# One encoder layer in float32r pieces: the up projection written in another order, and twelve additions of the third pass moved to VectorE

## The chip, the core and the metric

The kernel runs on one core of a Trainium2 chip. The metric is the time of the device in microseconds (us), the median over runs. The engines are PE (TensorE, matmuls), ACT (ScalarE), DVE (VectorE), POOL (GpSimd) and SP (SyncE, which here only issues DMAs).

## The reference

One layer: RMSNorm, one input projection, neighbourhood attention and a bidirectional gated recurrence side by side, a gated merge, then the MLP that the change touches, and a last RMSNorm:

```python
m = rms_norm(h, norm_mlp[l])                                   # h: 16 + 1024 rows of 1024, float32
h = h + jnp.square(jax.nn.relu(m @ w_up[l])) @ w_down[l]       # w_up 1024 x 4096, w_down 4096 x 1024
h = rms_norm(h, norm_final)                                    # the first 16 rows are dropped
```

## The kernel before

Every float32 matrix is split into a high part, `hi`, rounded to float32r by a cast on ACT, and a low part, `lo` = value - `hi`, made by a subtraction on DVE. A product is three matmuls: hi x hi, hi x lo and lo x hi. The low part is called the cast's remainder below. `weights` (L985 to L991) does this for a block of 128 x 512 weights: the cast at L989, the remainder at L990. It takes its tiles `wh`, `wl` in turn from one or two pools, with four buffers of each in each pool.

Both products of the MLP are done by Winograd's form of Strassen's scheme: 1024 rows and 1024 input columns are cut in two by two blocks, and seven products of half the size stand in place of eight. The up projection makes 4096 columns in 16 pairs of column blocks (`Pair`, m = 0 to 15). A pair has seven products, `product_1` to `product_7`. Each is a `chain` (L687 to L694) of 12 matmuls, four slices of the depth times three, that adds into one PSUM bank. The left sides are weights: the blocks a11, a12, a22 and the sums s1 to s4 that `pair_sums` makes on DVE (L682 to L685). The right sides are blocks of the normed rows and their sums (t1 to t4), transposed by PE.

Products 1 and 2 share a bank `pa`: p1 is copied to SBUF on ACT (L1055) between them, and their sum gives u11. Products 3 and 5 share `pc`: p3 is copied on ACT (L1065) before product 5 adds to the bank. Products 6, 7 and 4 share `pb`: after each, DVE adds p1 to the bank into a tile `uv` (L1070, L1085, L1100), and only then may the next chain add to the bank. DVE adds `pc` to u1 (L1074) and to u3 (L1091), and POOL subtracts p3 from u3 (L1086). Each result is relu'd and squared on ACT (L994, L995), and POOL makes four block sums of them for the next product (L1079); all go to DRAM tiles `usp`.

The order of all engines in this stage is as written: the code stands in a block that takes the scheduling out of the framework's hands (`manual_schedule`), so each engine does its instructions in the order in which the lines are called, and waits on semaphores for the other engines. Loads of weights and stores of blocks go through SP's queue in that order too.

The stage begins while the 20 transposes of the rows' last blocks and sums (L941, with a cast at L943 and its remainder at L944) are still to be done: each stands ahead of a slice of a chain. For this, products 1 and 2 of the first three pairs (`q.early`, EARLY = 3) are done before the loop over the pairs, with weights that are loaded apart (`first_load`, `first_weights`). So an early pair has five chains in the loop and a later one seven. In the loop product 4 of a pair is done in the next pair's turn. The last pair (`q.last`) makes its block sums on DVE and no weights for a next pair, but the first two steps of the down projection (`next_step`).

The down projection takes four passes over the pairs; eight banks are added to in a pass. Each step reads a pair's block from `usp` and a block of w_down, splits both (`split` at L95 to L97: cast L96, remainder L97) and has 24 matmuls. In the third pass a step makes one more difference of weights on DVE (L1268), and rows of results are added together beside it (`side`, L1334 to L1356).

Of the kernel before, what the change touches and what calls it, by code (L numbers as in the profile page):

```python
# [13 lines left out]
ALU = mybir.AluOpType  # L14
# [34 lines left out]
def layer(ctx: ExitStack, tc: tile.TileContext, x, meta, w_in, w_na, w_hg, w_o, w_up, w_dn,  # L49
# [478 lines left out]
    with (tc.tile_pool(name="npr", bufs=1, side="right", reuse_waits="tile") as npr,  # L528
# [18 lines left out]
        for p in range(NPAIR):  # L547
# [43 lines left out]
            for b in (0, 4, 8):  # L591
                pt = bank("t", "vpt")
                m = min(4, 9 - b)
# [102 lines left out]
    def up_bank(t):  # L696
        return bank(t, t).rearrange("p a b -> p (a b)")
# [254 lines left out]
    nB = []  # L952
# [32 lines left out]
    def weights(src):  # L985
        w_pools.append(w_pools.pop(0))
        hi, lo = (a_tile(w_pools[-1], t, F32R, 4) for t in ("wh", "wl"))
        v = (lambda t: t.rearrange("p (k c) -> p k c", c=P)) if len(src.shape) == 3 else (lambda t: t)
        act.copy(v(hi), src)  # L989
        dve.tensor_tensor(v(lo), src, v(hi).bitcast(F32), op=ALU.subtract)  # L990
        return hi, lo  # L991
# [10 lines left out]

    def first_weights(m):
        first_w[m] = [weights(first_raw[m][:, q:q + 4]) for q in (0, 4)]

# [44 lines left out]

    def product_1(q, w=None, between=lambda k: None):
        q.p1, q.u11 = a_tile(upa, "p1", bufs=EARLY), a_tile(upa, "u11", bufs=EARLY)
        q.pa = up_bank("pa")
        chain(q.pa, w or q.W["a11"], nV["b11"], True, between)
        act.copy(q.p1, q.pa)  # L1055
# [6 lines left out]
    def product_3(q):  # L1062
        q.pc, q.p3 = up_bank("pc"), a_tile(upb, "p3")
        chain(q.pc, q.W["s4"], nV["b22"], True)
        act.copy(q.p3, q.pc)  # L1065

# [4 lines left out]

    def product_5(q):
        chain(q.pc, q.W["s1"], nV["t1"], False)
        dve.tensor_tensor(q.u1, q.u1, q.pc, op=ALU.add)  # L1074
        relu2(q.u1, q.u1)

# [4 lines left out]

    def product_7(q):
        q.u3 = a_tile(upb, "uv", bufs=6)
        chain(q.pb, q.W["s3"], nV["t3"], False)
        dve.tensor_tensor(q.u3, q.pb, q.p1, op=ALU.add)  # L1085
        pool.tensor_tensor(q.u3, q.u3, q.p3, op=ALU.subtract)  # L1086

        block_out(q, 2, q.u11, q.u1, ALU.subtract, usp[2][q.m][:, 1])

    def finish_u3(q):  # L1090
        dve.tensor_tensor(q.u3, q.u3, q.pc, op=ALU.add)  # L1091
        relu2(q.u3, q.u3)
        (act if q.last else sp).dma_start(usp[2][q.m][:, 0], q.u3)
        block_out(q, 0, q.u1, q.u3, ALU.add, usp[1][q.m][:, 1])
        block_out(q, 1, q.S[0], q.u11, ALU.subtract, usp[1][q.m][:, 0])

    def product_4(q):
        u2 = a_tile(upb, "uv", bufs=6)
        chain(q.pb, q.W["a22"], nV["t4"], False)
        dve.tensor_tensor(u2, q.pb, q.p1, op=ALU.add)  # L1100
        relu2(u2, u2)
        (act if q.last else sp).dma_start(usp[0][q.m][:, 1], u2)
        block_out(q, 3, u2, q.S[1], ALU.subtract, usp[3][q.m // 2][:, q.m % 2])

    first_load(0)
    first_load(1)
    first_weights(0)
    first_weights(1)
    first_load(2)
    with tc.manual_schedule(engines={e.engine for e in (pe, act, dve, pool, sp)}):  # L1110
# [21 lines left out]
        rows_.close()  # L1132
        hress.close()
# [3 lines left out]
        load_pair(1)  # L1137
        product_1(pairs[2], first_w[2][0])
        pair_sums(pairs[0])
# [30 lines left out]
        product_4(pairs[-1])  # L1170
        next_step()

# [161 lines left out]
    def side(ps_, m):  # L1334
# [4 lines left out]
        if ps_ == 2 and 4 <= m < 12:  # L1339
            j = m // 2 - 2  # L1340
            if m % 2 == 0:
                pool.tensor_tensor(acc[j, 1], acc[j, 1], c5[j], op=ALU.add)
                pool.tensor_tensor(acc[j + 4, 1], acc[j + 4, 1], c5[j], op=ALU.add)
            else:
                pool.tensor_tensor(acc[j, 1], acc[j, 1], q1[j], op=ALU.add)
                square(j, 0)
# [106 lines left out]
```

## Time and profile before

| | us |
|---|---|
| median of 3 runs (1553.54 to 1555.42) | 1555.04 |
| the profiled execution's own time | 1555.45 |
| its span, first to last instruction | 1553.7 |
| busy in it: PE, DVE, ACT, POOL | 1504.5, 1040.5, 655.1, 412.4 |

The mean granted clock of PE is 0.995 of full speed. In what follows a row of the timeline reads: start and length in us, engine, line, operation, result<-operands, shapes, and in brackets how long the engine was idle before it and who released it. A matmul's length holds its way through the array, so matmuls overlap; how dense they are is seen from their starts. A row of waits reads: who waited, for whom, us in total, times, longest. Line numbers are those of the kernel before where the time is of before; in the changed kernel L1065 has become L1066, L1070 L1072, L1074 L1076, L1100 L1102, L1079 L1082, L1185 L1195, and L1268 L1278.

### The profile page before, as it was taken

To read this page: it belongs to the slowest core of one execution; us is meant where nothing else is said; L and a number is where in the kernel's file an instruction comes from. 1 tells how busy PE (TensorE), PEld (TensorE's weight loads), DVE (VectorE), ACT (ScalarE), POOL (GpSimd) and SP (SyncE) were. 2 spreads that over 40 slices of the span, in tenths; PEclk is the share of its full clock that TensorE was granted. 3 is DMA by queue.
4 is the path that set the end of the run, shared out by engine and by line. 5 is a ranking of instruction groups with operands and counts; after the bars stand their busy time and mean duration, and the time that the engine had idled before them with its cause. 6 is when DMAs were issued, how large, how long until landed. Compare 5 with 4: busy or idle time off the path is not lost. (4 is left out here: it accounts for less than half of the span.)

```text
span 1553.7 us, 23462 instructions
## 1 busy us (share of the span) xinstructions
PE 1504.5 (97%) x9188; PEld 1252.5 (81%) x9188; DVE 1040.5 (67%) x1589; ACT 655.1 (42%) x1173; POOL 412.4 (27%) x367
## 2 busy tenths in 40 slices
PE   6999999999999999999999999899999999999998
PEld 5788888877888887888888887788888888887886
DVE  6666666664876877666485367777777544879676
ACT  6231313124666666334133244444444443433444
POOL 4313131315314400011000122444444300237132
PEclk9999999999999999999999999999999999999999
DMA  5101010103123128434746123444444576562324
GB/s 180 42 28 56 28 56 29 56 28 127 50 72 119 62 68 264 136 129 161 252 163 216 55 89 109 147 153 151 150 151 154 203 270 237 195 230 98 106 82 149
DMA packets 142591, 196.13 MB, mean 126 GB/s; under 512 B 8064, under 2 KB 90112, under 8 KB 142480
## 3 DMA queue, kind: packets, MB, share of 16 engines
q1 hardware_dynamic: 133680, 173.13, 33.8%
q10 hardware_dynamic: 6624, 14.16, 2.3%
q0 software_dynamic: 2176, 7.34, 1.3%
q8 instruction: 72, 1.18, 0.3%
q14 instruction: 39, 0.32, 0.1%
HBM read 140.08 MB, written 54.53 MB: 125 GB/s over the span
## 5 line engine op out<-in xcount | busy, mean ns | idle before, releaser
L135 PE MATMUL mm<-aT,hi 128*128 128x512 f32 (+2 forms) x640 | 229.7, 359 | 2.1 <-DVE QX L563 1.5
L137 PE MATMUL mm<-aT,lo 128*128 128x512 f32 (+2 forms) x640 | 227.5, 356 | 0.0
L136 PE MATMUL mm<-aT,hi 128*128 128x512 f32 (+2 forms) x640 | 226.3, 354 | 0.0
L135 PEld LDWEIGHTS mm<-aT,hi 128*128 128x128 f32 x640 | 121.7, 190 | 16.4 <-issue 1.7
L97 DVE TENSOR_TENSOR dl<-ur,dh 128x1024 fp32r<-128x1024 f32 x54 | 75.5, 1398 | 85.5 <-ACT dh L96 85.4
L137 PEld LDWEIGHTS mm<-aT,lo 128*128 128x128 f32 x640 | 121.5, 190 | 13.3
L136 PEld LDWEIGHTS mm<-aT,hi 128*128 128x128 f32 x640 | 121.7, 190 | 12.5
L96 ACT CAST dh<-ur 128x1024 fp32r<-128x1024 f32 x54 | 56.9, 1053 | 161.0 <-issue 78.1
L990 DVE TENSOR_TENSOR wl<-raw,wh 128x512 fp32r<-128x512 f32 x50 | 55.5, 1115 | 45.2 <-ACT wh L989 45.2
L125 ACT CAST hi<-raw 128x1024 fp32r<-128x1024 f32 x36 | 37.8, 1050 | 106.1 <-PE mm L136 75.5
L994 ACT ACTIVATE uv<-uv 128x512 f32<-128x512 f32 x48 | 30.4, 632 | 118.2 <-DVE uv L1100 66.4
L990 DVE TENSOR_TENSOR wl<-sx,wh 128x512 fp32r<-128x512 f32 x70 | 48.0, 696 | 31.8 <-ACT wh L989 31.7
L1086 POOL TENSOR_TENSOR uv<-uv,p 128x512 f32<-128x512 f32 x16 | 25.9, 1619 | 141.9 <-ACT wh L989 105.5
L1265 POOL TENSOR_TENSOR w<-w,tt 128x512 f32<-128x512 f32 x16 | 23.4, 1462 | 131.1 <-DVE tt L1264 103.4
L399 POOL TENSOR_TENSOR Y<-X,TN 128x512 f32<-128x512 f32 x20 | 33.8, 1691 | 88.8 <-DVE X L396 88.8
L692 PE MATMUL pb<-nt,wh 128*128 128x512 f32 x128 | 51.4, 402 | 6.1 <-DVE uv L1085 3.8
L126 DVE TENSOR_TENSOR lo<-raw,hi 128x1024 fp32r<-128x1024 f32 x34 | 45.9, 1349 | 16.1 <-ACT hi L125 16.0
L618 DVE CUSTOM_DVE_ANT_0 pr<-nsc,NB 128x432 f32<-128x432 f32 (+1 forms) x64 | 35.2, 559 | 27.2 <-PE nsc L613 27.0
L92 POOL TENSOR_SCALAR rtm<-ssq 128x1 f32<-128x1 f32 (+1 forms) x17 | 6.6, 391 | 173.3 <-ACT junk L920 159.2
L692 PE MATMUL pa<-nT,wh 128*128 128x512 f32 x128 | 51.5, 402 | 0.7 <-ACT p L1055 0.7
L1175 PE MATMUL mm<-dl,dh 128*128 128x512 f32 x124 | 49.1, 396 | 1.9 <-DVE dl L97 1.9
L135 PE MATMUL mm<-wh,mT 128*128 128x512 f32 x128 | 50.2, 392 | 0.0
(380 smaller groups left out, 4449.8 us busy)
## 6 DMA issues: line engine op xcount, KB each, us to landing
raw<-in_w_in SPq DMA_DIRECT2D x56, 512.0 KB, 4.0
ur<-usp SPq DMA_DIRECT2D x54, 512.0 KB, 3.5
raw<-in_w_up SPq DMA_DIRECT2D x16, 1024.0 KB, 6.6
usp<-us SPq DMA_DIRECT2D x60, 256.0 KB, 4.6
sg<-gsp SPq DMA_DIRECT2D x16, 512.0 KB, 3.7
w<-in_w_dn SPq DMA_DIRECT2D x16, 512.0 KB, 4.6
usp<-uv SPq DMA_DIRECT2D x30, 256.0 KB, 5.7
gsp<-gv ACTq DMA_DIRECT2D x24, 256.0 KB, 2.6
```

What stands on the lines that cost most here:

```text
L96: act.copy(hi, src)
L97: dve.tensor_tensor(lo, src, hi.bitcast(F32), op=ALU.subtract)
L125: act.copy(hi[:, :kc], raw[:, :kc])
L126: eng.tensor_tensor(lo[:, :kc], raw[:, :kc], hi[:, :kc].bitcast(F32), op=ALU.subtract)
L135: pe.matmul(ps, lh, rh, start=first, stop=False)
L136: pe.matmul(ps, lh, rl, start=False, stop=False)
L137: pe.matmul(ps, ll, rh, start=False, stop=last)
L399: pool.tensor_tensor(fap(Y, h, mid3), fap(X, h, mid3), fap(TT, 0, [[4, g], [n + 3, 2], [0, h]]), op=ALU.mult)
L618: dve.tensor_tensor_reduce(out=pr[:, :w], in0=sc[:, :w], in1=NB[:, i, o:o + w], scale=1.0, scalar=3.0e38, op0=ALU.add, op1=ALU.min, accum_ ...
L692: pe.matmul(ps, lhs[0][:, c], rhs[0][:, k], start=first and k == 0, stop=False, skip_group_check=True)
L990: dve.tensor_tensor(v(lo), src, v(hi).bitcast(F32), op=ALU.subtract)
L1175: pe.matmul(ps, a[n == 2][:, q, j * P:(j + 1) * P], b[n == 1][:, q], start=first and n == 0, stop=last and n == 2, skip_group_check=True)
```

## The change

1. *p1 - p3 ahead, in the result's tile.* p3 is copied into the tile of u3, and POOL makes u3 = p1 - u3 there at once (L1066, L1067). After product 7 DVE adds `pb` (L1087) and `pc` (L1088). Before, DVE added p1 to `pb` (L1085), POOL subtracted p3 (L1086), and DVE added `pc` (L1091) in the next pair's turn.
2. *Casts ahead of activations.* The cast and remainder of s3 stand ahead of u1's relu and square, those of a22 ahead of u3's. In the early pairs s1 goes ahead of product 5. In a later pair s1 does as well. u2's relu and square come after the weights a11 and s4 (early) or ahead of product 3 (later).
3. *Block sums and loads.* A pair's first three block sums stand together behind product 7 (`pair_out`), so the next load of weights stands behind their stores in SP's queue. For the last pair they come behind product 4.
4. *Three p1 chains first.* Ahead of the loop the order is product 1 of pairs 0, 1, 2 and then product 2 of pairs 0, 1, 2. The third p1 has a bank of its own (`mm`). The first slice has no transposes ahead of it. Transposes stand in the first four chains, as before in the first four.
5. *Third pass.* Three additions for each of four row blocks go from POOL to DVE (L1342, L1343, L1345 before).

```diff
-    def first_weights(m):
-        first_w[m] = [weights(first_raw[m][:, q:q + 4]) for q in (0, 4)]
+    def first_weights(m, *halves):
+        first_w.setdefault(m, []).extend(weights(first_raw[m][:, 4 * q:4 * q + 4]) for q in halves)
...
     def product_3(q):
-        q.pc, q.p3 = up_bank("pc"), a_tile(upb, "p3")
+        q.pc, q.u3 = up_bank("pc"), a_tile(upb, "uv", bufs=6)
         chain(q.pc, q.W["s4"], nV["b22"], True)
-        act.copy(q.p3, q.pc)
+        act.copy(q.u3, q.pc)
+        pool.tensor_tensor(q.u3, q.p1, q.u3, op=ALU.subtract)
...
-    def product_5(q):
+    def product_5(q, then):
         chain(q.pc, q.W["s1"], nV["t1"], False)
         dve.tensor_tensor(q.u1, q.u1, q.pc, op=ALU.add)
+        then()
         relu2(q.u1, q.u1)
...
-    def product_7(q):
-        q.u3 = a_tile(upb, "uv", bufs=6)
+    def product_7(q, then):
         chain(q.pb, q.W["s3"], nV["t3"], False)
-        dve.tensor_tensor(q.u3, q.pb, q.p1, op=ALU.add)
-        pool.tensor_tensor(q.u3, q.u3, q.p3, op=ALU.subtract)
-
-        block_out(q, 2, q.u11, q.u1, ALU.subtract, usp[2][q.m][:, 1])
-
-    def finish_u3(q):
+        dve.tensor_tensor(q.u3, q.u3, q.pb, op=ALU.add)
         dve.tensor_tensor(q.u3, q.u3, q.pc, op=ALU.add)
+        then()
         relu2(q.u3, q.u3)
         (act if q.last else sp).dma_start(usp[2][q.m][:, 0], q.u3)
+
+    def pair_out(q):
+
+        block_out(q, 2, q.u11, q.u1, ALU.subtract, usp[2][q.m][:, 1])
         block_out(q, 0, q.u1, q.u3, ALU.add, usp[1][q.m][:, 1])
         block_out(q, 1, q.S[0], q.u11, ALU.subtract, usp[1][q.m][:, 0])
...
-        product_1(pairs[0], first_w[0][0], lambda k: transposes(1))
-        transposes(1)
+        product_1(pairs[0], first_w[0][0], lambda k: transposes(k > 0))
+        first_weights(2, 0)
+        transposes(2)
         scale_row(7, rs7)
-        product_2(pairs[0], first_w[0][1], lambda k: transposes(1))
-        nB.append(row_sums(3))
-        transposes(1)
         product_1(pairs[1], first_w[1][0], lambda k: transposes(1))
         transposes(1)
-        first_weights(2)
-        product_2(pairs[1], first_w[1][1], lambda k: transposes(1))
+        nB.append(row_sums(3))
+        product_1(pairs[2], first_w[2][0], lambda k: transposes(1), "mm")
         transposes(1)
+        product_2(pairs[0], first_w[0][1], lambda k: transposes(1))
+        transposes(1)
+        first_weights(2, 1)
+        product_2(pairs[1], first_w[1][1])
...
             (product_3 if q.early else product_1)(q)
-            if m:
-                finish_u3(pairs[m - 1])
             if m + 1 < NP:
                 pair_sums(pairs[m + 1])
             if m:
                 product_4(pairs[m - 1])
             if q.early:
                 product_6(q)
-                next_weights(m, "a11", "s4", "a12", "s2")
+                next_weights(m, "a11", "s4")
+                if m:
+                    finish_u2(pairs[m - 1])
+                next_weights(m, "a12", "s2", "s1")
             else:
+                finish_u2(pairs[m - 1])
                 product_3(q)
                 next_weights(m, "a11", "s4")
                 product_2(q)
                 next_weights(m, "a12", "s2")
                 product_6(q)
-            product_5(q)
-            next_weights(m, "s1")
-            product_7(q)
-            next_weights(m, "s3", "a22")
-        finish_u3(pairs[-1])
+                next_weights(m, "s1")
+            product_5(q, lambda: next_weights(m, "s3"))
+            product_7(q, lambda: next_weights(m, "a22"))
+            if not q.last:
+                pair_out(q)
         product_4(pairs[-1])
+        finish_u2(pairs[-1])
...
             if m % 2 == 0:
-                pool.tensor_tensor(acc[j, 1], acc[j, 1], c5[j], op=ALU.add)
+                dve.tensor_tensor(acc[j, 1], acc[j, 1], c5[j], op=ALU.add)
```

What this does to the order of single engines is shown at three places.

DVE in the turn of pair 0 and at the start of pair 1's, before (`uv` are u1, u3, u2, `wl` the remainders, `sx` the sums of the weights):

```order
L1070 TENSOR_TENSOR uv<-pb,p_9186 128x512
L990 TENSOR_TENSOR wl<-sx,wh 128x512 x2
L1074 TENSOR_TENSOR uv<-uv,pc 128x512
L990 TENSOR_TENSOR wl<-sx,wh 128x512
L1085 TENSOR_TENSOR uv<-pb,p_9186 128x512
L990 TENSOR_TENSOR wl<-sx,wh 128x512
L990 TENSOR_TENSOR wl<-raw,wh 128x512
L1091 TENSOR_TENSOR uv<-uv,pc 128x512
L682 TENSOR_TENSOR sx<-raw 128x512
```

And in the changed kernel, the same place:

```order
L1072 TENSOR_TENSOR uv<-pb,p_9186 128x512
L990 TENSOR_TENSOR wl<-sx,wh 128x512 x3
L1076 TENSOR_TENSOR uv<-uv,pc 128x512
L990 TENSOR_TENSOR wl<-sx,wh 128x512
L1087 TENSOR_TENSOR uv<-uv,pb 128x512
L1088 TENSOR_TENSOR uv<-uv,pc 128x512
L990 TENSOR_TENSOR wl<-raw,wh 128x512
L682 TENSOR_TENSOR sx<-raw 128x512
```

The third remainder (s1) has moved ahead of L1076 and s3's ahead of L1087, the second addition to u3 follows the first at once, and one remainder, not two, stands between it and the sums.

PE where the output projection ends (`mm`) and the stage begins (`pa` is the bank of p1, `pt` that of transposes), before:

```order
L137 MATMUL mm<-wh_8478,mT_8427 128x512
L941 MATMUL pt<-ident,hres_8493 128x128 x4
L692 MATMUL pa<-nT_8818,wh 128x512
L693 MATMUL pa<-nT_8819,wh 128x512
L694 MATMUL pa<-nT_8818,wl 128x512
```

and in the changed kernel:

```order
L137 MATMUL mm<-wh_8478,mT_8427 128x512
L692 MATMUL pa<-nT_8818,wh 128x512
L693 MATMUL pa<-nT_8819,wh 128x512
L694 MATMUL pa<-nT_8818,wl 128x512
L941 MATMUL pt<-ident,hres_8493 128x128 x4
```

Three matmuls of the first chain now stand ahead of the first four transposes.

DVE in the third pass, two steps (`hr` are rows of the result, `w` the difference of weights), in the changed kernel; before, the same place holds only the rows of L1268 (now L1278) and L97:

```order
L97 TENSOR_TENSOR dl<-w_5_12065,dh 128x1024
L1352 TENSOR_TENSOR hr<-hr,c_11988 128x512
L1353 TENSOR_TENSOR hr<-hr,c_11988 128x512
L1278 TENSOR_TENSOR w_6_12109<-w_6_12109 128x512
L97 TENSOR_TENSOR dl<-ur,dh 128x1024
L97 TENSOR_TENSOR dl<-w_6_12109,dh 128x1024
L1355 TENSOR_TENSOR hr<-hr,q_11984 128x512
L1278 TENSOR_TENSOR w_7_12149<-w_7_12149 128x512
```

Two additions have come into one step and one into the next.

More of the change, by code (lines that the diff above doesn't have):

```diff
@@ L1049, in next_weights, with product_1 @@
                 q.W[v] = weights(q.A[v])
-    def product_1(q, w=None, between=lambda k: None):
+    def product_1(q, w=None, between=lambda k: None, tag="pa"):
         q.p1, q.u11 = a_tile(upa, "p1", bufs=EARLY), a_tile(upa, "u11", bufs=EARLY)
-        q.pa = up_bank("pa")
+        q.pa = up_bank(tag)
         chain(q.pa, w or q.W["a11"], nV["b11"], True, between)
@@ L1097, in product_4, with finish_u2 @@
     def product_4(q):
-        u2 = a_tile(upb, "uv", bufs=6)
+        q.u2 = a_tile(upb, "uv", bufs=6)
         chain(q.pb, q.W["a22"], nV["t4"], False)
[L1100 to L1103, printed above, removed]
+        dve.tensor_tensor(q.u2, q.pb, q.p1, op=ALU.add)
+    def finish_u2(q):
+        relu2(q.u2, q.u2)
+        (act if q.last else sp).dma_start(usp[0][q.m][:, 1], q.u2)
+        if q.last:
+            pair_out(q)
+        block_out(q, 3, q.u2, q.S[1], ALU.subtract, usp[3][q.m // 2][:, q.m % 2])
     first_load(0)
     first_load(1)
-    first_weights(0)
-    first_weights(1)
+    first_weights(0, 0, 1)
+    first_weights(1, 0, 1)
     first_load(2)
@@ L1137, in layer @@
         load_pair(1)
-        product_1(pairs[2], first_w[2][0])
         pair_sums(pairs[0])
@@ L1341, in side @@
             if m % 2 == 0:
-                pool.tensor_tensor(acc[j, 1], acc[j, 1], c5[j], op=ALU.add)
-                pool.tensor_tensor(acc[j + 4, 1], acc[j + 4, 1], c5[j], op=ALU.add)
+                dve.tensor_tensor(acc[j, 1], acc[j, 1], c5[j], op=ALU.add)
+                dve.tensor_tensor(acc[j + 4, 1], acc[j + 4, 1], c5[j], op=ALU.add)
             else:
-                pool.tensor_tensor(acc[j, 1], acc[j, 1], q1[j], op=ALU.add)
+                dve.tensor_tensor(acc[j, 1], acc[j, 1], q1[j], op=ALU.add)
                 square(j, 0)
```

1 line of the change is left out of this document (added).

## The prediction

> **What bounds the kernel now.** I read the page first, then the waits of the matmul engine (PE), then its timeline by stage.
>
> ```profile
> span 1553.7 us, 23462 instructions
> ...
> PE 1504.5 (97%) x9188; PEld 1252.5 (81%) x9188; DVE 1040.5 (67%) x1589; ACT 655.1 (42%) x1173; POOL 412.4 (27%) x367
> ```
>
> PE is busy for 97% of the span, so an edit can save what PE loses by waiting, and only if nothing else becomes late. The waits of PE in the stages that the change touches (us in total, times, longest):
>
> ```profile
> PE pb L692 <- DVE uv L1085: 3.8, 2, 2.5
> PE pb L692 <- DVE uv L1070: 2.1, 2, 1.3
> PE mm L1175 <- DVE dl L97: 1.9, 5, 0.7
> PE pt L941 <- DVE hres L898: 0.8, 1, 0.8
> PE pa L692 <- ACT p L1055: 0.7, 1, 0.7
> PE pb L1185 <- DVE uv L1100: 0.5, 1, 0.5
> ```
>
> They hold 9.8 us, and each costs more than its row says, since PE starts slowly after one. What is really lost in the pair loop comes from PE's timeline: the first matmul of the loop, two chain starts, and the first matmul behind the last pair's product 7.
>
> ```profile
> 939.24 0.39 PE L692 MATMUL pc<-nT,wh 128*128 128x512 f32 x1
> 1226.26 0.39 PE L692 MATMUL pb<-nT,wh 128*128 128x512 f32 x1
> 1228.98 0.39 PE L692 MATMUL pc<-nt,wh 128*128 128x512 f32 x1
> 1234.42 0.39 PE L1185 MATMUL mm<-wh 128*128 128x512 f32 x1
> ```
>
> A chain of 12 matmuls takes 1228.98 - 1226.26 = 2.72 us. From 939.24 to 1234.42 PE runs 105 chains (16 pairs of seven, less products 1 and 2 of the three early pairs and less the last product 4): 105 x 2.72 = 285.6 us of work in 295.2 us. So 9.6 us are lost there, and that is the most the loop can give. Where it is lost, in the second early pair (p7, p4 and so on are the products):
>
> ```profile
> 961.31 0.50 PE L692 MATMUL pb<-nt,wh 128*128 128x512 f32 x1
> 965.21 0.63 ACT L994 ACTIVATE uv<-uv 128x512 f32<-128x512 f32 x1 [2.19 <-DVE uv L1074]
> 967.04 0.69 DVE L990 TENSOR_TENSOR wl<-sx,wh 128x512 fp32r<-128x512 f32 x1 [1.87 <-ACT wh L989]
> 967.65 0.68 DVE L1085 TENSOR_TENSOR uv<-pb,p 128x512 f32<-128x512 f32 x1
> 968.39 0.50 PE L692 MATMUL pb<-nt,wh 128*128 128x512 f32 x1 [1.31 <-DVE uv L1085]
> 970.56 0.67 DVE L1091 TENSOR_TENSOR uv<-uv,pc 128x512 f32<-128x512 f32 x1
> 971.15 1.19 DVE L682 TENSOR_TENSOR sx<-raw 128x512 f32<-128x512 f32 x1
> 974.68 1.77 DVE L685 TENSOR_TENSOR sx<-raw,sx 128x512 f32<-128x512 f32 x1
> 976.98 0.68 DVE L1070 TENSOR_TENSOR uv<-pb,p 128x512 f32<-128x512 f32 x1
> 977.71 0.50 PE L692 MATMUL pb<-nt,wh 128*128 128x512 f32 x1 [0.86 <-DVE uv L1070]
> ```
>
> Product 7 starts at 961.31 and is through by 964.0. VectorE (DVE) takes its bank over only at 967.65 (L1085), because ahead of that it waits 1.87 us for a weight cast which on ScalarE (ACT) stands behind two activations of 0.63 us each (965.21 is the first). So p4, due at 964.0 + 2.7 = 966.7, starts at 968.39. Then the four sums of the next weights take until 976.4, and L1070 at 976.98 makes p7 late (977.71). The sums are slow because of GpSimd (POOL):
>
> ```profile
> 972.65 1.57 POOL L1079 TENSOR_TENSOR us<-uv 128x512 f32<-128x512 f32 x1 [0.86 <-ACT uv L995]
> 945.50 0.69 DVE L685 TENSOR_TENSOR sx<-raw,sx 128x512 f32<-128x512 f32 x1
> 946.10 0.68 DVE L1070 TENSOR_TENSOR uv<-pb,p 128x512 f32<-128x512 f32 x1
> ```
>
> With nothing on POOL a sum takes 0.69 us (945.50). Beside POOL's work it takes 1.77 (974.68), that is 1.1 more, while L1091, which reads a PSUM bank, stays at 0.67 (970.56).
>
> **The change part by part.** I sum against the profiled execution's 1555.45 us (span 1553.7 and 1.75 around it), which lies 0.41 above the median of the three runs, 1555.04.
>
> *Pair loop.* Each pair keeps the same chains on PE, 14 DVE operations in an early pair, and five on POOL. p1 - p3 is made on POOL as soon as p3 is copied, two chains ahead of its reader or more. With time 0 at the end of p7, the early pair goes on DVE: L1087 from 0.2 (the last matmul's 0.39 less the 0.227 from one start to the next; a PSUM read, 0.67), L1088 0.67, the cast's remainder 0.69, four sums at their slow price 5.3 (971.15 to 976.4), L1102 0.68: done at 8.2. L1072 then waits for p6, which ends at 3 x 2.72 = 8.2, and is through by 9.1; p7 begins at 10.9. p4 begins at 2.72 and needs L1087, done at 0.9. Both waits that PE now has get 1.8 us of room. Three weight remainders (2.0) and L1076 follow until 11.8, s3 until 12.5, and the next L1087 is due at 13.8: DVE is in time. The casts that stand ahead of the activations cost PE nothing as long as the activations behind them, 1.3 us a time, fit into the rest of the 13.6 us (five chains): only POOL and the stores read what they make.
>
> In pairs 3 to 15 a pair has seven chains, 19.0 us, for the same sums and two more casts, so there is more room still. The copy of p1 is due at three chains, 8.2, and follows L1088 (done at 1.6), two activations (2.9) and a copy of 0.6: 3.5. If that cover went, PE would wait ahead of p2.
>
> The first pair is the exception, as no product 4 stretches it:
>
> ```profile
> 937.37 0.69 DVE L685 TENSOR_TENSOR sx<-raw,sx 128x512 f32<-128x512 f32 x1
> 938.09 1.14 ACT L989 CAST wh<-sx 128x512 fp32r<-128x512 f32 x2 [1.76 <-DVE sx L685]
> 942.67 0.58 ACT L1065 COPY p<-pc 128x512 f32<-128x512 f32 x1
> ```
>
> There POOL is free now (L1070 at 946.10 follows undisturbed sums), and p7 starts at 939.24 + 3 x 2.72 = 947.4. Afterwards POOL's p1 - p3 starts behind the copy (942.67 + 0.58) and makes one sum 1.1 longer: L1072 ends near 947.5 instead of 946.8, against a p7 that is due 0.3 earlier, at 947.1. I take 0.6 us lost there, between 0 (the operations miss each other) and 1.7 (two sums hit). Another 0.4 us I leave for slow restarts. The loop gives 9.6 - 0.6 - 0.4 = 8.6 us.
>
> *Three p1 chains first.* The first three matmuls (3 x 2.72/12 = 0.68) fill most of the 0.8 us that PE waits on L898, and the 0.7 us wait for the copy of p1 goes, since two other chains lie between. So PE could be at the loop 1.36 us earlier, at 937.9. What is late next is s4: its sum ends at 938.06 (937.37 + 0.69), its cast at 938.66. DVE starts the sums 0.7 earlier but has a weight remainder (0.6) moved ahead of them, so the sum ends near 937.95, the cast near 938.6, and with the remainder the loop starts near 938.9. Gain 0.3, from 1.3 (no wait for s4) to -0.4 (the first matmuls wait like the transposes). The extra cast in the first chain lies beside transposes.
>
> *Last pair.* L1102 and what follows it no longer stand behind three block sums, so the 0.5 us wait at L1185 goes, with its restart 0.6. Two matmuls fewer stand ahead of product 4 (4 x 0.227 = 0.9 us instead of 1.36); L1087 needs 0.9 of it. The stores of u1 and u3 wait longer, but nobody reads those blocks before later passes.
>
> *SP's queue.* The load of the next weights now stands behind two block stores, and so behind POOL.
>
> ```profile
> raw<-in_w_up SPq DMA_DIRECT2D x16, 1024.0 KB, 6.6
> ```
>
> In an early pair it goes out near 6 instead of 1 and lands 6.6 later, at 12.6 to 13; the sums that read it start at 13.6 + 2.2 = 15.8. So 2 to 3 us of cover; in the later pairs 19.0 - 13.6 = 5.4 more. I cost it at nothing.
>
> *Third pass.* POOL's twelve additions run beside DVE. First the window (length, then each engine's busy time and count, PE's first), then DVE's rows beside POOL (four) and alone (three):
>
> ```profile
> 1400.00:1450.00 50.00, 48.49 (x212) 38.98 (x211) 45.11 (x32) 21.47 (x24) 30.53 (x17) 1.00 0.30 106
> ```
>
> ```profile
> 1419.25 1.77 DVE L1268 TENSOR_TENSOR w<-w 128x512 f32<-128x512 f32 x1
> 1420.95 2.31 DVE L97 TENSOR_TENSOR dl<-ur,dh 128x1024 fp32r<-128x1024 f32 x1
> 1423.18 2.31 DVE L97 TENSOR_TENSOR dl<-w,dh 128x1024 fp32r<-128x1024 f32 x1
> 1425.41 1.77 DVE L1268 TENSOR_TENSOR w<-w 128x512 f32<-128x512 f32 x1
> 1438.16 1.22 DVE L97 TENSOR_TENSOR dl<-ur,dh 128x1024 fp32r<-128x1024 f32 x1 [0.83 <-ACT dh L96]
> 1439.30 1.22 DVE L97 TENSOR_TENSOR dl<-w,dh 128x1024 fp32r<-128x1024 f32 x1
> 1440.44 0.68 DVE L1268 TENSOR_TENSOR w<-w 128x512 f32<-128x512 f32 x1
> ```
>
> Beside POOL one step takes DVE 1425.41 - 1419.25 = 6.16 us, and PE's step of 24 matmuls is 24 x 0.227 = 5.44, so DVE sets the pace until 1436. Alone it is 1.14 + 1.14 + 0.68 = 3.0. With two additions on DVE (at most 0.7 each, as a sum) it is 4.4, with one 3.7, both under 5.44 with room even for one slowing of 1.1. In 1400 to 1450 PE made 212 matmuls where 50 / 0.227 = 220 fit: 8 x 0.227 = 1.9 us come back. POOL loses only work that nobody waits for.
>
> The page "Perfetto Trace Analysis" of the Trainium skill, section "Optimizing Scalar/DVE Operations", says of the port that the two engines share that moving operations between them "might not help". By that this term would be 0 and not 1.9; the rows of DVE alone and beside POOL speak for 1.9.
>
> Sum: 8.6 + 0.3 + 0.6 + 1.9 = 11.4. 1555.45 - 11.4 = 1544.05, and 0.41 less against the median, 1543.6; I say 1544. All waits gone and no new one would be 9.6 + 1.3 + 0.6 + 1.9 = 13.4: 1541.6. With the bad ends (1.7 in place of 0.6, -0.4 in place of 0.3) it is 9.6: 1545.4; an unseen wait of 0.1 us per pair would add 1.6: 1547.
>
> **The rivals.**
>
> 1. *The early pairs stay late* (0.12). The loads miss their 2 to 3 us of cover, or POOL hits more DVE operations than four sums. For it: an early pair moves as many bytes in 13.6 us as a later one in 19. Against: the trace's landing time above. Then the 5.9 us of the first two rows of PE's waits stay lost: 1543.6 + 5.9 = 1549.5, from 1547.5 (a third of them goes all the same) to 1550.5 (another microsecond lost elsewhere).
>
> 2. *The third pass gives nothing* (0.08), the additions being as dear on DVE as beside it: 1543.6 + 1.9 = 1545.5. The uncontended rows speak against it.
>
> 3. *Slower, by ACT's queue* (0.04). In pairs 3 to 15 eight weight tiles serve seven weights a pair, so the cast of s3 waits for p5 and that of a22 for p7, and now the activations and the copy of p1 queue behind them. The copy has 8.2 - 3.5 = 4.7 us before p2 needs it. Only from there each further microsecond costs 13 pairs one each: 13 x 1.1 = 14.3 against the 11.4 gained, 1558 (1555.04 + 2.9). It needs ACT 5.8 us behind in every pair, and nothing in the rows gives more than the 1.3 of two activations.
>
> 4. *The waits only move* (0.08): with PE closer behind, the casts are late at other chains and the loop keeps what it loses; without its 8.6 us the time is 1552.2.
>
> **How the numbers follow.** The sum has 0.68. The range takes it from 1541 (all waits gone, 1541.6, less a third of the 1.9 us between the shown runs, 1553.54 and 1555.42) up to rival 1's 1550.5. It leaves out rivals 3 and 4 and a little of the rest. About 0.2%, 3.1 us, is what a measurement of this kernel can tell from no change. Faster by more than that, under 1551.9: the sum and rivals 1 and 2, 0.88. Within it: rival 4, 0.08. Slower: rival 3, 0.04.
>
> **What would show it.** In the changed profile PE's waits on the DVE operations of p7 and p4 in pairs 1 to 3 should be gone, but for one near 0.5 us in the first pair; the loop from its first pc matmul to L1195 should last about 286.6 us; the window of the third pass should hold 219 or 220 matmuls in 50 us, with L1278 and both casts' remainders at 0.7 and 1.2. The sum is wrong if the loop still takes over 290 us, if L1072 comes later than 10.9 us behind p7's end, or if the sums wait for a load of weights.

## The result, and the profile after

The changed kernel takes 1541.29 us (median of 4 runs, 1539.05 to 1543.87) against 1555.23 before (4 runs, 1553.54 to 1555.59): a ratio of 0.9913, with a 95% interval from 0.9892 to 0.9934, so 10 to 17 us less. The profiled execution took 1543.13 us, 12.3 less than the profiled one of before; the medians differ by 13.9, and the 1.6 between them is scatter of the kind shown below. The page's first rows of the changed kernel:

```profile
span 1541.4 us, 23453 instructions
...
PE 1500.9 (97%) x9188; PEld 1253.1 (81%) x9188; DVE 1030.8 (67%) x1601; ACT 658.0 (43%) x1173; POOL 386.7 (25%) x355
```

PE's waits from the last chains of the output projection to the handoff, of the changed kernel (who, for whom, us, times, longest):

```profile
PE pc L692 <- ACT wh L989: 0.6, 1, 0.6
PE pb L692 <- DVE uv L1072: 0.2, 1, 0.2
```

The waits on L1085, L898, the copy of p1 and L1100 are gone, and of those on L1070 (now L1072) 0.2 us is left. One is new, the 0.6 for s4's cast, which the prediction named as the next to be late. The landmarks in the timeline: the last L898 (the residual's addition, behind which this stage runs but for its first three matmuls), the loop's first matmul, the fourth product 7, the first L1195.

```profile
911.85 0.69 DVE L898 TENSOR_TENSOR hres<-hres,mm 128x512 f32<-128x512 f32 x1 [3.52 <-PE mm L137]
938.42 0.50 PE L692 MATMUL pc<-nT,wh 128*128 128x512 f32 x1 [0.62 <-ACT wh L989]
994.11 0.50 PE L692 MATMUL pb<-nt,wh 128*128 128x512 f32 x1 [0.24 <-DVE uv L1072]
1225.44 0.39 PE L1195 MATMUL mm<-wh 128*128 128x512 f32 x1
```

The same L898 starts at 911.95 in the profile of before:

```profile
911.95 0.69 DVE L898 TENSOR_TENSOR hres<-hres,mm 128x512 f32<-128x512 f32 x1 [3.53 <-PE mm L137]
```

So the loop takes 1225.44 - 938.42 = 287.02 us instead of 295.18, and the way from L898 to the loop 26.57 instead of 939.24 - 911.95 = 27.29. The window of the third pass (PE's busy time and count first; the last three numbers are the clock, DMA share, GB/s):

```profile
1387.00:1437.00 50.00, 50.00 (x222) 41.27 (x221) 37.45 (x37) 22.09 (x26) 10.27 (x6) 1.00 0.32 113
```

PE is busy for all 50 us, with 222 matmuls instead of 212.

**Why stretches, and not whole times, are compared below.** Up to L898 all kernels here are the same program, yet that row starts anywhere from 906.89 to 912.80 us in their profiles: the scatter of several us from run to run lies there. From L898 on two executions of the changed kernel agree within 0.03 us, and two of e6 within 0.04; the loop of before, untouched in e1, came out 0.48 apart. So a difference under some 0.5 us between two single profiles isn't taken as an effect below unless something else supports it. In this table each stretch is a difference of the starts of such rows: the last L898, the loop's first `pc` matmul, the first `mm` matmul of the handoff (L1195 in the changed kernel), the last matmul, and the end of the span.

| us | L898 to loop | loop | loop's end to last matmul | L898 to end of span |
|---|---|---|---|---|
| before | 27.29 | 295.18 | 311.86 | 641.75 |
| changed | 26.57 | 287.02 | 308.50 | 629.55 |
| third pass alone (e1) | 27.30 | 295.66 | 309.50 | 639.88 |
| loop alone (e2) | 27.31 | 286.88 | 311.15 | 632.71 |
| casts behind (e3) | 26.56 | 309.16 | 308.46 | 651.54 |
| p3 late (e4) | 26.57 | 287.46 | 308.54 | 630.00 |
| first stage back (e5) | 27.31 | 286.84 | 308.74 | 630.28 |
| three more moves (e6, e11) | 25.48, 25.48 | 286.94, 286.94 | 308.53, 308.51 | 628.35, 628.31 |
| four DVE operations more (e7) | 26.60 | 296.20 | 308.50 | 638.73 |
| six DVE operations more (e8) | 26.57 | 321.57 | 308.52 | 664.03 |
| casts alone (e9) | 27.31 | 285.99 | 311.51 | 632.22 |
| changed, once more (e10) | 26.57 | 287.00 | 308.57 | 629.52 |
| four more moves (e12) | 25.48 | 287.97 | 308.45 | 629.35 |

### The profile page after: what moved, and what is told of

Same layout as the page of the kernel before. It is cut to its first block, busy times and chain, and to the rows that moved or that the text cites. A ratio compares the mean times of both kernels' runs of the same rounds, so it can differ in the third digit from the quotient of the medians.

```text
span 1541.4 us, 23453 instructions
## 1 busy us (share of the span) xinstructions
PE 1500.9 (97%) x9188; PEld 1253.1 (81%) x9188; DVE 1030.8 (67%) x1601; ACT 658.0 (43%) x1173; POOL 386.7 (25%) x355
## 4 chain that ended last, share of the span: by engine, by line
PE 87%; DVE 6%; issue 2%; ACT 2%; DMA 1%; POOL 1%; SPq 0%; POOLq 0%; ACTq 0%; DVEq 0%
PE mm L135 11%; PE mm L136 10%; PE mm L137 10%; PE mm L1185 5%; PE pa L1185 4%; PE pb L692 4%; PE pb L694 4%; PE pb L693 4%; PE pb L1185 4%; PE pc L1185 4%; PE pc L692 3%; PE pc L694 3%; PE pc L693 3%; PE pa L694 2%; PE pa L692 2%
## 5 line engine op out<-in xcount | busy, mean ns | idle before, releaser
L97 DVE TENSOR_TENSOR dl<-ur,dh 128x1024 fp32r<-128x1024 f32 x54 | 71.0, 1316 | 87.3 <-ACT dh L96 87.1
L990 DVE TENSOR_TENSOR wl<-raw,wh 128x512 fp32r<-128x512 f32 x50 | 41.0, 823 | 36.5 <-ACT wh L989 36.3
L990 DVE TENSOR_TENSOR wl<-sx,wh 128x512 fp32r<-128x512 f32 x70 | 61.0, 882 | 3.4 <-ACT wh L989 3.3
L989 ACT CAST wh<-sx 128x512 fp32r<-128x512 f32 x70 | 42.2, 620 | 42.2 <-PE pc L693 23.9
L692 PE MATMUL pb<-nt,wh 128*128 128x512 f32 x128 | 50.2, 392 | 0.3 <-DVE uv L1072 0.2
L693 PE MATMUL pb<-nt,wh 128*128 128x512 f32 x128 | 49.8, 389 | 0.0
L694 PE MATMUL pb<-nt,wl 128*128 128x512 f32 x128 | 49.8, 389 | 0.0
```

Source lines behind the costliest of these rows:

```text
L97: dve.tensor_tensor(lo, src, hi.bitcast(F32), op=ALU.subtract)
L692: pe.matmul(ps, lhs[0][:, c], rhs[0][:, k], start=first and k == 0, stop=False, skip_group_check=True)
L693: pe.matmul(ps, lhs[0][:, c], rhs[1][:, k], start=False, stop=False, skip_group_check=True)
L694: pe.matmul(ps, lhs[1][:, c], rhs[0][:, k], start=False, stop=k == 3, skip_group_check=True)
```

## The experiments

My theory: the loop loses because VectorE waits in its queue for casts that stand behind activations on ACT; and the parts of the change add up. Rivals: that p1 - p3, ready ahead, is what closed the gaps; that waits only move; that additions cost the same on either of the engines which share a port.

**The third pass alone (e1).** Before, with the three additions on DVE:

```diff
-                pool.tensor_tensor(acc[j, 1], acc[j, 1], c5[j], op=ALU.add)
+                dve.tensor_tensor(acc[j, 1], acc[j, 1], c5[j], op=ALU.add)
```

(and so for the other two.)

> The kernel before, with the third pass's twelve additions on VectorE and nothing else changed. My theory: the additions cost DVE 0.7 us each and take POOL's slowing (1.1 us an operation) away, so the 2.3 us of gaps that PE has in that pass close and the window of 50 us holds 220 matmuls and not 212: 1.9 to 2.5 us faster than before, about 1553.0. Rival (moving work between the two engines that share a port gives nothing): 1555.2, within 0.5 us, the window still at 212 or the gaps at other matmuls.

1551.25 us (11 runs) against 1555.00 (17), a ratio of 0.9978 (0.9970 to 0.9987). From the loop's end to the last matmul it is 2.36 us less than before; the loop, which this edit doesn't touch, came out 0.48 longer, so from L898 to the end 1.87 is left. The window of the third pass in this kernel:

```profile
1396.50:1446.50 50.00, 50.00 (x222) 41.21 (x221) 37.79 (x39) 21.11 (x24) 8.19 (x5) 1.00 0.33 108
```

222 matmuls, as in the changed kernel. The rival is out, and with it the "might not help" of the Trainium skill's "Perfetto Trace Analysis", section "Optimizing Scalar/DVE Operations", for this place: eight of the twelve additions take 0.68 us on DVE and four 1.78 (L1345, beside a POOL operation of another line), and in return the slowings of 1.1 us on the operations beside POOL's additions go.

**The loop alone (e2) and the first stage taken back (e5).** e2 is before with the change of the loop only. e5 is the changed kernel with the order of before ahead of the loop:

```diff
-        product_1(pairs[0], first_w[0][0], lambda k: transposes(k > 0))
-        first_weights(2, 0)
-        transposes(2)
+        product_1(pairs[0], first_w[0][0], lambda k: transposes(1))
+        transposes(1)
...
```

> The kernel before, with the new order of the pair loop alone; the three p1 chains and the third pass stay as before. My theory: the parts add up, so the loop gives its 8.2 us (as the profile of the changed kernel shows), and the handoff behind it 0.6: 1546.4. Rival (the loop is fast only because the work ahead of it now starts it earlier, so that part of the gain belongs to the three p1 chains): less than 7 us, over 1548.

> The changed kernel, with the chains and casts ahead of the pair loop in the order of before (the three p1 chains undone). The stretch from DVE's fourth hres addition (L898) to the end lasts 687.65 us in the changed kernel and 699.85 before; the third pass alone took 1.87 off it and the loop alone 9.04, so 1.3 is left for this part. My theory: the parts add up and the stretch is 1.3 us longer (0.8 to 1.4), some 1542.5 in all; PE again waits 0.7 us on L898 and 0.7 on the copy of p1. Rival (the new wait for s4's cast takes back nearly all of it, the 0.3 that the forecast gave it): 0.3 us longer.

e2: 1543.30 us (5 runs) against 1555.00, 0.9930 (0.9918 to 0.9943). The stretch is 9.04 us shorter than before, the loop alone 8.30 and the handoff 0.71. e5: 1542.49 (5 runs) against 1552.46 (15) on its chip, 0.9939 (0.9926 to 0.9951). Its stretch is 0.73 us longer than the changed kernel's, just under "0.8 to 1.4" and far from the rival's 0.3, all of it ahead of the loop (0.74). With the third pass (2.36) and the loop's 9.04 that makes 12.13 of 12.20: the parts add up (11.64 with e1's whole stretch, 1.87, in place of 2.36).

**Which half of the loop's change does it (e3, e4, e9).** e3 puts the activations of products 5 and 7 ahead of the casts again, e4 makes p1 - p3 late again:

```diff
-        then()
         relu2(q.u1, q.u1)
+        then()
...
-        act.copy(q.u3, q.pc)
-        pool.tensor_tensor(q.u3, q.p1, q.u3, op=ALU.subtract)
+        act.copy(q.p3, q.pc)
...
-        dve.tensor_tensor(q.u3, q.u3, q.pb, op=ALU.add)
+        dve.tensor_tensor(q.u3, q.pb, q.p1, op=ALU.add)
+        pool.tensor_tensor(q.u3, q.u3, q.p3, op=ALU.subtract)
```

(the first piece, and the same for u3, is e3; the others are e4.)

> The changed kernel, with the activations of products 5 and 7 again ahead of the casts of s3 and a22; p1 - p3 stays ahead. My theory: the cast of s3 comes 1.3 us later on ACT, and VectorE, which waits for it in its queue ahead of L1087 and again ahead of the sums, runs about 2 us late at L1087 and 3.8 late at L1072 in each early pair, against the 1 to 1.8 us of room there; the two waits come back in pairs 1 to 3, and the kernel loses 5 us (3 to 8). Rival (what closed the gaps is that p1 - p3 is ready): 0 to 1 us lost.

> The changed kernel, with p3 again in a tile of its own and subtracted on POOL behind product 7; the casts stay ahead of the activations. My theory: VectorE waits 1.8 us for POOL ahead of L1088 and gets one sum back undisturbed (1.1), so L1072 comes 0.7 us later in an early pair and product 7 is late by about a microsecond in pairs 2 and 3: 1.5 us lost (0.5 to 3). Rival (p1 - p3 made ahead is what closed the gaps): 5 us or more lost.

e3: 1563.46 us (6 runs), 1.0055 (1.0041 to 1.0069): slower than before, and its stretch is 22 us longer than the changed kernel's where 5 were expected. The direction was right and the size wrong, since I had counted the early pairs only. A later pair of e3 on DVE:

```profile
1100.82 0.68 DVE L1072 TENSOR_TENSOR uv<-pb,p 128x512 f32<-128x512 f32 x1
...
1104.57 1.37 DVE L990 TENSOR_TENSOR wl<-sx,wh 128x512 fp32r<-128x512 f32 x1 [1.87 <-ACT wh L989]
1105.87 0.67 DVE L1087 TENSOR_TENSOR uv<-uv,pb 128x512 f32<-128x512 f32 x1
1106.58 0.69 DVE L1088 TENSOR_TENSOR uv<-uv,pc 128x512 f32<-128x512 f32 x1
1109.14 1.37 DVE L990 TENSOR_TENSOR wl<-raw,wh 128x512 fp32r<-128x512 f32 x1 [1.87 <-ACT wh L989]
...
1120.93 0.68 DVE L1072 TENSOR_TENSOR uv<-pb,p 128x512 f32<-128x512 f32 x1
```

Two waits of 1.87 us for casts, each behind two activations that themselves start with the addition just ahead. From L1072 to L1072 it is 20.11 us where PE needs 7 x 2.72 = 19.04, and nowhere in that round does DVE wait for PE. What PE waits for in that kernel:

```profile
PE pb L692 <- DVE uv L1072: 11.0, 14, 1.3
PE pb L692 <- DVE uv L1087: 5.5, 3, 2.8
```

e4: 1542.79 us (5 runs), 0.9920 (0.9908 to 0.9932). Its stretch is 0.45 us longer than the changed kernel's, just under "0.5 to 3" and no more than the loop of before differed by between two profiles. Yet DVE now waits for POOL in 15 of the 16 pairs (in e4 L1088 is POOL's subtraction and L1089 DVE's addition of `pc`; us in total, times, longest):

```profile
DVE uv L1089 <- POOL uv L1088: 21.7, 15, 1.5
```

21.7 us of waiting cost 0.45 at most. In the later pairs they lie where DVE has room (e7 and e8 measure it). In an early pair it has none, but there the wait is paid back. The first two rows are of e4, the third of the changed kernel at the same place:

```profile
967.13 0.69 DVE L1089 TENSOR_TENSOR uv<-uv,pc 128x512 f32<-128x512 f32 x1 [1.41 <-POOL uv L1088]
...
972.82 0.68 DVE L685 TENSOR_TENSOR sx<-raw,sx 128x512 f32<-128x512 f32 x1
```

```profile
971.04 1.77 DVE L685 TENSOR_TENSOR sx<-raw,sx 128x512 f32<-128x512 f32 x1
```

In the changed kernel POOL's p1 - p3 of the next pair slows the fourth sum; in e4 nothing of POOL runs beside it, and DVE's round is 14.11 us against 14.07. So e9 asked whether the order on ACT is enough by itself. It is before, with DVE's order untouched (`then` is the cast and remainder of s1, `finish_u2` holds u2's activations, store and block sum):

```diff
         dve.tensor_tensor(q.u1, q.u1, q.pc, op=ALU.add)
+        then()
         relu2(q.u1, q.u1)
...
                 next_weights(m, "a11", "s4", "a12", "s2")
+                if m:
+                    finish_u2(pairs[m - 1])
```

> The kernel before, with ScalarE's order alone changed in the pair loop: the casts of a11, s4, a12 and s2 go ahead of the activations of u2 in the early pairs, and the cast of s1 ahead of the activations of u1. VectorE's order, POOL's p3 subtraction and the third pass stay as before. My theory (the waits for casts are the cause, not the place of p1 - p3): VectorE's 1.28 and 1.87 us of waiting in an early pair go, its round of 16.4 us falls under PE's 13.6, and the pair loop lasts 287 to 288.5 us instead of 295.2; 7 us faster (6 to 8.3). Rival (VectorE's turn at u3, which waits for POOL's subtraction and comes in the next pair, keeps the loss): 1 to 4 us faster.

1542.87 us (5 runs) against 1554.91 (9), 0.9927 (0.9914 to 0.9939). The loop takes 285.99 us, 9.2 less than before and 1.0 less than in the changed kernel: the whole 105 x 2.72 = 285.6 without a gap. That is more than the "6 to 8.3" expected. The 1.0 rests on one profile of e9 against two of the changed kernel (287.02 and 287.00). DVE's waits for casts in the loop, one row each of before, the changed kernel, e3 and e9:

```profile
DVE wl L990 <- ACT wh L989: 74.8, 45, 3.2
```

```profile
DVE wl L990 <- ACT wh L989: 39.1, 28, 3.2
```

```profile
DVE wl L990 <- ACT wh L989: 94.0, 48, 2.9
```

```profile
DVE wl L990 <- ACT wh L989: 44.3, 29, 3.2
```

The two long loops (295 and 309 us) go with 75 and 94 us of such waits, the two short ones (287 and 286) with 39 and 44. The totals don't count alike: 29 to 31 us in each kernel are waits of 2.4 in the later pairs for a11's cast, which stands behind u2's activations in all four and, from the fifth pair on, holds up nothing on PE in the changed kernel and e9. What differs are waits of 1.8 to 1.9 us for a cast behind two activations that have just begun: 16 before, 1 in the changed kernel, 31 in e3, none in e9. An early pair of e9, ACT (two casts, and u2's relu behind them) and then DVE (L1086 is L1085 of before):

```profile
956.04 1.14 ACT L989 CAST wh<-sx 128x512 fp32r<-128x512 f32 x2 [3.93 <-DVE sx L685]
957.09 0.63 ACT L994 ACTIVATE uv<-uv 128x512 f32<-128x512 f32 x1
```

```profile
956.53 0.67 DVE L1070 TENSOR_TENSOR uv<-pb,p 128x512 f32<-128x512 f32 x1
...
960.79 0.69 DVE L1086 TENSOR_TENSOR uv<-pb,p 128x512 f32<-128x512 f32 x1 [0.41 <-PE pb L694]
...
966.13 1.78 DVE L684 TENSOR_TENSOR sx<-raw 128x512 f32<-128x512 f32 x1
967.83 1.77 DVE L685 TENSOR_TENSOR sx<-raw,sx 128x512 f32<-128x512 f32 x1
...
970.13 0.67 DVE L1070 TENSOR_TENSOR uv<-pb,p 128x512 f32<-128x512 f32 x1
```

Both casts are ahead of u2's activations, DVE runs into a wait for PE (0.41) instead of one for ACT, and its round is 13.60 us, PE's own pace. The last two sums are as slow beside POOL as before (1.78 and 1.77), so it isn't that POOL's work moved out of the way. So the theory holds in a stronger form than I had it: the order on ACT is the cause, and p1 - p3 ahead isn't needed for the gain.

**How much room DVE has (e7, e8).** The changed kernel, with s3's remainder made again four or six times behind the first in pairs 3 to 14:

```diff
-            product_5(q, lambda: next_weights(m, "s3"))
+            product_5(q, lambda: (next_weights(m, "s3"), again(m)))
```

> The changed kernel, with four more VectorE operations (the remainder of s3 made again) behind s3's remainder in every pair from the fourth to the last but one: 4 x 0.60 = 2.4 us more in VectorE's queue. My theory: in a late pair VectorE waits 1.14 and 1.50 us for PE, 2.64 in all, and everything else in its round of 19.0 us is its own work or waits for ACT, so 2.4 us cost nothing: within 1 us of the changed kernel. Rival (VectorE isn't what sets the pace in the kernel with the casts behind the activations; late weights do): also nothing here.

> As the kernel with four more VectorE operations, but with six: 3.6 us more. My theory: 3.6 - 2.64 = 1.0 us too much, so a late pair takes 20.0 us and not 19.0, PE waits on L1072 in each, and 12 pairs cost 11 to 12 us: about 1553. Rival (late weights, not VectorE's queue, cost 1.07 us a pair when the casts stood behind the activations): under 3 us.

Both expectations failed. e7: 1550.64 us (10 runs) against 1552.46, 0.9988 (0.9977 to 0.9998), with a loop 9.2 us longer than the changed kernel's. e8: 1575.51 (4 runs), 1.0158 (1.0144 to 1.0173), its loop 34.6 us longer. DVE in e7 (L1099 are the operations added) and PE behind it:

```profile
1092.89 3.85 DVE L1099 TENSOR_TENSOR wl<-sx,wh 128x512 fp32r<-128x512 f32 x4
1096.66 0.68 DVE L1087 TENSOR_TENSOR uv<-uv,pb 128x512 f32<-128x512 f32 x1
```

```profile
1097.39 0.50 PE L692 MATMUL pb<-nt,wh 128*128 128x512 f32 x1 [0.42 <-DVE uv L1087]
```

The four take 1096.66 - 1092.89 = 3.77 us and not 2.4, because a block sum on POOL (1.79 us) runs beside them. In the changed kernel DVE waits in such a round for PE twice, and that is all its room, with 0.22 for a cast:

```profile
1108.68 0.69 DVE L1076 TENSOR_TENSOR uv<-uv,pc 128x512 f32<-128x512 f32 x1 [1.14 <-PE pc L694]
1111.47 0.69 DVE L1087 TENSOR_TENSOR uv<-uv,pb 128x512 f32<-128x512 f32 x1 [1.50 <-PE pb L694]
```

The 2.40 us of waiting for a11's cast in the same round are no room: that cast follows DVE's own L1102 by way of u2's activations, and in e7 the wait is 2.40 again. 1.14 + 1.50 + 0.22 = 2.86; 3.77 - 2.86 = 0.9 too much, and PE's pairs come 19.80 apart (1117.19 less 1097.39, the same matmul a pair later) instead of 19.04, 0.8 longer. In e8:

```profile
1102.90 5.30 DVE L1099 TENSOR_TENSOR wl<-sx,wh 128x512 fp32r<-128x512 f32 x6
1108.12 0.68 DVE L1087 TENSOR_TENSOR uv<-uv,pb 128x512 f32<-128x512 f32 x1
```

The six take 1108.12 - 1102.90 = 5.22 us, 2.4 too much, and PE loses 2.1 in each wait. The count of room was right, the price per operation wrong. The rest of e8's loss is the clock, below.

**Beyond the change (e6, e11, e12).** e6 aims at what PE still loses: the cast of pair 2's second weights and the last four transposes go ahead of the activations, L1072 of the first pair between two sums, L1072 of a later pair ahead of a12's and s2's remainders. e12 also puts L1072 of an early pair ahead of L1102.

```diff
-        product_2(pairs[0], first_w[0][1], lambda k: transposes(1))
-        transposes(1)
-        first_weights(2, 1)
+        def last_four(k):
+            transposes(1 + k // 3)
+            if k == 3:
+                first_weights(2, 1)
+
+        product_2(pairs[0], first_w[0][1], last_four)
...
                 product_2(q)
-                next_weights(m, "a12", "s2")
                 product_6(q)
-                next_weights(m, "s1")
+                next_weights(m, "a12", "s2", "s1")
```

> The changed kernel, and three more moves of the same kind: the last four transposes and the cast of the second half of pair 2's first weights go ahead of the last matmuls and the activations of the first product 2, so that the sums and s4's cast come about 0.9 us earlier; in the first pair VectorE's L1072 goes between the second and third sum; in the later pairs L1072 goes ahead of the remainders of a12 and s2. My theory: the gaps that PE still has there (0.3 and 1.2 us at the loop's start, 0.4 at the first product 7, 0.5 at the fourth) close and no other opens: 2.0 us less in the stretch from L898 to the end (1.0 to 2.4), some 1539.3. Rival (waits only move: VectorE's other work is late by as much at the next chain): within 0.5 us of the changed kernel.

> The kernel with three more moves once more. Its first profile had 628.35 us from the last L898 to the end, 1.2 less than the changed kernel, and not the 2.0 expected: the gaps at the loop's start closed, those at the products 7 moved to later chains. Theory: 628.4 again (within 0.5), and its time 1.2 us under that of the changed kernel on the same chip. Rival: no difference between them that outlasts the scatter.

> The changed kernel once more, on the chip of the kernels that it is compared with here. Theory: from the last L898 to the end of the span 629.5 us, as in its first profile (within 0.5); whatever the whole times scatter by, several us from run to run, lies ahead of that. Rival: the scatter is in the changed part, and this stretch differs by over 1 us.

> The kernel with three more moves, and L1072 of an early pair ahead of L1102 of the pair before it. VectorE's round in the early pairs is 14.06 us against PE's 13.6, so it falls behind by 0.46 a pair; the swap gives product 7 another 0.6 us of room. Theory: the gap of 0.29 and 0.11 at the third product 7 closes, that at the third product 4 (0.33 and 0.10) stays, since L1088 comes as late as before: 628.0, 0.4 less (0.2 to 0.8). Rival: nothing closes, as the round is the limit, 628.4.

e6: 1539.62 us (5 runs) against 1552.46, 0.9923 (0.9909 to 0.9936). On one chip, with before at 1554.91: e11, the same kernel, 1540.15 (4 runs, 1537.00 to 1541.29), 0.9903 (0.9889 to 0.9916); the changed kernel once more (e10) 1542.31 (5 runs, 1540.06 to 1544.57), 0.9919 (0.9906 to 0.9931). The whole times overlap; the stretch of e10 is that of the first profile, and e6's and e11's are 1.2 us shorter (2.0 were expected). Nearly all of that comes from the way to the loop (1.09); in the loop, 0.08 shorter, the gaps only moved, since DVE's round in an early pair is the longer one. e12: 1542.64 (5 runs), 0.9917 (0.9903 to 0.9930), and its loop is 1.0 us longer than e11's. There L1102 comes 0.6 later, so u2's activations do, and so the casts behind them (line numbers of that kernel are 1 to 3 higher: L990 is a cast, L991 a remainder, L1088 the first addition to u3):

```profile
975.58 1.43 DVE L991 TENSOR_TENSOR wl<-raw,wh 128x512 fp32r<-128x512 f32 x1 [0.72 <-ACT wh L990]
```

```profile
980.07 0.50 PE L693 MATMUL pb<-nt,wh 128*128 128x512 f32 x1 [1.22 <-DVE uv L1088]
```

DVE's waits for the casts of pairs 1 and 2, 1.27 and 0.72 us where e11 has 0.68 and 0.1, became 1.22 for PE at a product 4. Neither theory had this: it is the same fault as in before, a cast behind activations, made anew. The fastest kernel that ran is e6 (e11). One with ACT's order of e9 in place of the rest of the loop's change, and the other parts as in e6, would by the rows of the table have 25.48 + 285.99 + 308.5 + 7.4 (the last matmul to the end) = 627.4: an estimate, it wasn't tried.

## Why the prediction came out, point by point

The sum was 11.4 us less and the stretch shows 12.20: 0.72 ahead of the loop, 8.16 in it, 3.36 behind it, less 0.04 at the end. So 0.8 of what the median fell below the forecast (1543.6 before rounding, 1541.29 measured) was gained in the changed part. The other 1.5 is scatter, and that the median still lies in the range, 0.3 above its lower end, is partly luck.

*Pair loop: a gain of 8.6 forecast (286.6 us), 8.16 measured (287.02).* The size was right (1.4 us of the 9.6 stay lost and not 1.0); of the mechanism, half. "The casts that stand ahead of the activations" is the cause (e3, e9). p1 - p3 "two chains ahead of its reader", which the argument put first, is worth 0.45 at most (e4), and the casts alone get a faster loop without it.

*"Both waits that PE now has get 1.8 us of room."* Wrong for L1072. DVE's and PE's rows at the products 7 of pairs 1 and 2:

```profile
959.27 0.68 DVE L1072 TENSOR_TENSOR uv<-pb,p 128x512 f32<-128x512 f32 x1
...
961.22 2.05 DVE L990 TENSOR_TENSOR wl<-sx,wh 128x512 fp32r<-128x512 f32 x2 [0.68 <-ACT wh L989]
...
965.10 0.69 DVE L1088 TENSOR_TENSOR uv<-uv,pc 128x512 f32<-128x512 f32 x1
965.75 1.38 DVE L990 TENSOR_TENSOR wl<-raw,wh 128x512 fp32r<-128x512 f32 x1
...
973.34 0.68 DVE L1072 TENSOR_TENSOR uv<-pb,p 128x512 f32<-128x512 f32 x1
```

```profile
961.02 0.39 PE L692 MATMUL pb<-nt,wh 128*128 128x512 f32 x1
...
974.62 0.39 PE L692 MATMUL pb<-nt,wh 128*128 128x512 f32 x1
```

L1072 ends at 959.95 and 974.02, so the room is 1.07 and 0.60, and in pair 3 PE waits 0.24. DVE's round is 973.34 - 959.27 = 14.07 us where PE's is 13.6: the count left out that a22's remainder runs beside POOL (1.38 and not 0.69), and that a cast behind u2's activations still makes DVE wait (0.68). The first pair lost 0.36 of the 0.6 forecast, pair 3 0.5 that was not.

*Three p1 first: 0.3 forecast, 0.72.* What was late next is s4, as said. But I let the loop wait for the remainder too; PE's first two matmuls need only the cast, and the third lost 0.15.

*Last pair: 0.6 forecast,* 0.71 in e2. *Third pass: 1.9 forecast, 2.36 in e1.* I had taken 220 matmuls as the full window; it is 222. The "at most 0.7 each" is wrong for four of the twelve additions (1.78), but a step has room for "one slowing of 1.1", as said.

*SP's queue: nothing, and so it was.* A load of the second pair's turn and the first sum that reads it:

```profile
956.94 0.39 SPq L1016 DMA_DIRECT2D raw<-in_w_up  x1
```

```profile
967.04 0.68 DVE L682 TENSOR_TENSOR sx<-raw 128x512 f32<-128x512 f32 x1
```

This load landed 6.5 us after its issue, so 3.6 us of cover remain.

*Rival 3 was closer than its 0.04.* It asked for 5.8 us on ACT "in every pair" and held that nothing gives more than 1.3. By DVE's queue two waits of 1.87 against 2.86 of room are enough: e3 is that case, and slower than before. The later pairs have "more room still", but not enough for two such waits. With the new order on DVE, casts behind activations cost more than with the old one: 94.0 us of waits in e3, 74.8 in before.

*The other rivals.* The waits of the early pairs are gone, so neither rival 1 ("stay late") nor rival 4 ("only move") came about, but for the 0.2 at L1072; rival 2 is out by e1.

## What to carry to other kernels

Where two engines take turns (an activation that needs VectorE's sum, a cast that VectorE needs), put on the feeder's queue first what the other engine will wait for, and last what only a store reads; 21.7 us of waiting where there was room, or where it spared a slowing, cost at most 0.45 us; 3.74 us a pair where there was too little cost 22. Count the room of an engine as its waits for the bottleneck in one round, and price what is put there as it runs beside its neighbours, not alone. When whole times scatter more than the effect, compare stretches that start behind the scatter.

## What the runs showed of the hardware

The granted clock of PE halved behind some short waits, and not behind others as long. In e8 PE waits 1.9 us in each of 12 pairs; behind five of them its matmuls come 0.43 us apart instead of 0.23 for some 3.4 us. The window of one such patch, and one behind an equal wait without it (PE's busy time and count, then the granted clock as the third number from the end):

```profile
1087.60:1091.00 3.40, 3.40 (x10) 2.69 (x9) 3.37 (x4) 0.90 (x2) 2.82 (x2) 0.52 0.53 200
1108.90:1112.00 3.10, 3.10 (x14) 2.57 (x15) 3.06 (x5) 1.74 (x3) 1.07 (x1) 1.00 0.09 37
```

The 12 gaps of 2.14 us, restarts included (25.7 us), and five patches of some 1.7 us (8.5) make 34.2 of the 34.6 us of e8. The wait of 2.50 us in the profile of before had no such patch behind it, nor had one of 2.79 in e3, while one of 1.98 there had (granted clock 0.50 from 968.0 to 971.4, some 1.6 of e3's 22 us). What decides isn't shown. The Trainium skill, "TensorE: Matmul & The Clock Gate", section "HAM oscillation — how this bites in real kernels", gives the rule that PE should not idle for over some 3.4 us; here the clock halved behind gaps of 1.9 us five times in twelve, so keeping to that rule was not enough.

The slowing beside POOL follows the operands. In the changed kernel this block sum

```profile
965.28 1.29 POOL L1082 TENSOR_TENSOR us<-u,uv 128x512 f32<-128x512 f32 x1 [3.16 <-ACT uv L995]
```

runs beside two of the rows above: L1088 at 965.10, which reads a PSUM bank and one tile of SBUF, took 0.69 us as ever, and the remainder at 965.75, which reads two tiles of SBUF, 1.38. The Trainium skill says so too ("SBUF — State Buffer", section "Who interferes with whom": a VectorE instruction with two SBUF inputs contends with a GpSimd instruction that reads SBUF, one with at most one SBUF input, outside the modes that use two ports, doesn't), and these rows agree.
